# A fused decoder layer on one core: the first dilated head's transposes moved four half items later, and the last norm's inverse root taken from ScalarE and VectorE

## The chip, the core and the metric

The kernel runs on one core of a Trainium2 chip. The core has a matrix engine (TensorE, PE in the profile; its weight loads are listed as PEld), a vector engine (VectorE, DVE), a scalar engine (ScalarE, ACT), a general engine (GpSimd, POOL) and SyncE (SP), which here does nothing but issue transfers. Each engine works through a list of its own in order and waits on semaphores for the others. Transfers (DMA) are issued by SP, by GpSimd and in a few places by ScalarE; each of these has a queue of its own. The metric is the device time of one execution in microseconds (us).

## The reference, cut to what matters

One layer with batch 1, 512 tokens and width 1024, all in fp32. Three attention branches work in parallel, their outputs are gated and merged, and then come a norm, an MLP and a second norm:

```python
proj = x @ w_in                                  # q, k, v of three branches, gates
o_da = diff_attention(...)                       # 4 heads, two softmax maps each
o_sb = stick_breaking_attention(...)             # 8 heads
o_dl = dilated_attention(...)                    # 4 head slots x 3 groups
merged = sum(sigmoid(gate_i) * (o_i @ w_branch_i))
x = layer_norm(alpha * x + merged @ w_out, ln1_g, ln1_b)
c = square(relu(x @ w_up)) @ w_down              # 1024 -> 4096 -> 1024
ple = sigmoid(x @ w_ple_gate) * (p @ w_ple)
x = layer_norm(alpha * x + c + ple, ln2_g, ln2_b)
```

In the dilated branch three groups of keys (windows of 128, 512 and 2048 at strides of 1, 4 and 16) have a softmax each, and the outputs of the three are combined by their denominators:

```python
logits = where(valid, q @ k.T * dh ** -0.5 + bias, -inf)    # per group
lse = logsumexp(logits); o = exp(logits - lse) @ v
wts = softmax(stack(lses)); out = sum_g wts[g] * o[g]
```

The norm is the usual one; the inverse root in it is what the second part of the change computes in another way:

```python
mu = x.mean(-1); var = square(x - mu).mean(-1)
y = (x - mu) * rsqrt(var + 1e-5) * g + b
```

## The kernel before, in words

**Split products.** fp32 matrices are multiplied in pieces. A matrix is split into a high part (rounded, type fp32r) and the remainder, and a product is the sum of three matmuls: high by high, high by remainder, remainder by high. The weights come in blocks of 128 x 1024. SP loads them into a ring of buffers named `raw`; ScalarE casts the high part `wh` (L214), VectorE subtracts it to get the remainder `wl` (L216). A cast may begin only when TensorE has done its last matmul on the older weights in that place of the ring.

**Items.** The heavy work is a list of `items`. An item is a set of weight blocks, a function that emits its matmuls into a bank of PSUM (TensorE's accumulators), and an evacuation that copies or adds the bank into SBUF. The main loop goes through the list: it splits the blocks that come next, emits the evacuation of the item before, then the matmuls of this one. PSUM has two banks named `mm` and six named `at`.

**Value products.** The values of the dilated groups are computed by `value_pair` with a scheme of seven block products in place of eight, in the order 2, 1, 7, 6, 4, 5, 3, each for two halves of the tokens. One such item is twelve matmuls (L426 to L428: high by high, high by remainder, remainder by high, four times). The inputs of products 7, 6, 4 and 5 are sums and differences of blocks of x, made by the generator `value_forms`: VectorE subtracts (L369, L394 and their neighbours; tiles `fr`), ScalarE casts the high part (L239; `u7h`, `u6h` and so on), VectorE takes the remainder (L240; `u5l` and so on). L437 is a copy of a finished bank by ScalarE, L440 an addition by VectorE. After the seven products come ordinary value products on `xhT`, which is x itself.

**Side work.** The attention heads are Python generators. Beside the items the main loop calls `step()`, which moves each active generator on to its next `yield`; it is called before an item, and in the longer items again in the middle. An item of `value_pair` counts as half an item (size 0.5) and has one step, so that there one yield is one half item of twelve matmuls. What a generator emits in a step lies in each engine's list at that place, between the matmuls of the item. A helper then orders each engine's list; it can move single instructions against the order in which they were written.

**A dilated head.** `dil_head(hd)` makes the logits of its three groups, takes the exponentials, and combines the denominators: a matmul with `fold` and a few small VectorE instructions (L1646 to L1655; `mxx`, `ex`, `ot`), in the middle an exponential on ScalarE (L1650). The result `mxx` scales the eight tiles of probabilities: four `L0` tiles (L1657) and four `L12` tiles (L1661). Then TensorE transposes them, seven tiles for `pt0` (L1676, into two banks: five and two by the order of TensorE's list) and eight for `pt12` (L1685), and later multiplies them with the values (L1697, L1702). Between the scaling and the transposes stands one `yield` in every head, and for head 0, the first to run, two more, that is, three half items in all.

**The MLP and the last norm.** The MLP goes through 4096 hidden columns in eight parts up (L1010 copies a part of `up` out of PSUM) and down (L1076 to L1078). The last matmuls fill four token blocks; the last block is done in three pieces, listed in `ends`. When the third piece has been added and its statistics taken, `last_norm` runs (L1213): VectorE aggregates the statistics (L1216), adds epsilon (L1218), GpSimd takes the power -0.5 (L1219), while VectorE subtracts the mean and multiplies by the gain in two halves (L1221). Then three instructions multiply by the root and add the offset (L1224), each followed by its own transfer out (L1226), which is issued by SP, ScalarE and SP.

**Tables of ScalarE.** ScalarE's functions come from tables that have to be loaded. The kernel loads one at the start, and one more in the middle, for the sigmoid of the gates (L507). The root of the norms is taken by GpSimd throughout.

**Loads by GpSimd.** Sums of weight blocks for the seven-product schemes are made in memory by accumulating transfers on GpSimd's queue (L914, L916), all through the kernel. `lows` is the list of all weight remainders in the order in which they were emitted.

Of the kernel before, what the change touches and what calls it, by code (L numbers as in the profile page):

```python
# [14 lines left out]
OP = mybir.AluOpType  # L15
# [42 lines left out]
def trunk(tc, a, out):  # L58
    nc = tc.nc
    es = ExitStack()  # L60
    with es:
# [1094 lines left out]
        def plain(cs, c2, c4, kept):  # L1156

            sums, held = {}, []
            s6 = slot("bn6e")[:, :18].rearrange("p (a b) -> p a b", b=6)

            ends = [(0, slice(0, 512)), (1, slice(0, 256)), (1, slice(256, 512))]

            def part(tt, half, cc):
                n = cc.stop - cc.start
                r = tt % 2
                p, cp = {(0, 0): (2, c2), (1, 0): (4, c4)}.get((tt // 2, half), (0, []))

                def mm(ps):
                    for c, m in zip(cp, (5, 6)):
                        down_mm(ps, m, p, r, c, p == 2 and m == 5, False)  # L1170
                    for i in range(4):
                        h, lo = left[ND - 1, tt // 2, i % 2]
                        q = slice((i // 2) * 256 + r * P, (i // 2) * 256 + r * P + P)
                        c = cs[i % 2, half]
                        s = slice((i // 2) * 512 + cc.start, (i // 2) * 512 + cc.stop)
                        nc.tensor.matmul(ps[:, :n], h[:, q], c["h"][:, s], start=i == 0 and not p, stop=False,
                                         skip_group_check=True)
                        nc.tensor.matmul(ps[:, :n], h[:, q], c["l"][:, s], start=False, stop=False,
                                         skip_group_check=True)
                        nc.tensor.matmul(ps[:, :n], lo[:, q], c["h"][:, s], start=False, stop=i == 3,  # L1180
                                         skip_group_check=True)

                def ev(ps):
                    t = acc[tt, half]
                    if tt < 3:
                        if not half:
                            sums[tt] = small("lsm", 2)
                        nc.vector.scalar_tensor_tensor(t, t, 1.0, ps, op0=OP.mult, op1=OP.add,
                                                       accum_out=sums[tt][:, half:half + 1])
                        if half:  # L1190
                            def fin(h, y):
                                (nc.sync if h else nc.scalar).dma_start(
                                    out[0, tt * P:tt * P + P, 512 * h:512 * h + 512], y)
                            rest = layer_norm_act([acc[tt, 0], acc[tt, 1]], sums[tt], "ln2_g", "ln2_b", fin)
                            if tt == 2:
                                held.append(rest)
                            else:
                                rest()
                        return
                    i = nc.vector.tensor_add(t[:, cc], t[:, cc], ps[:, :n])  # L1200
                    if held:
                        with tc.issue_after(getattr(i, "ins", i)):
                            held.pop()()
                    nc.vector.bn_stats(s6[:, ends.index((half, cc)), :], t[:, cc])
                    if (half, cc) == ends[2]:
                        last_norm()
                free = list(cp) if p and r else []
                if (tt, half, cc) == (3, *ends[2]):
                    free = list(cs.values())
                item(free, mm, ev, need=list(cs.values()) + list(cp),  # L1210
                     bank=(lambda: kept["y", r]) if p == 4 else at_bank if tt == 3 else None)

            def last_norm():  # L1213
                ts = [acc[3, 0], acc[3, 1]]
                mv = small("mv", 2)
                nc.vector.bn_aggr(mv, s6)  # L1216
                r = small("lr", 1)
                nc.vector.tensor_scalar(r, mv[:, 1:2], EPS, None, op0=OP.add)  # L1218
                nc.gpsimd.tensor_tensor(r, r, mhalf, OP.pow)  # L1219
                for h in range(2):  # L1220
                    nc.vector.scalar_tensor_tensor(ts[h], ts[h], mv[:, 0:1], lnc["ln2_g"][h], op0=OP.subtract,  # L1221
                                                   op1=OP.mult)
                for i, (h, cc) in enumerate(ends):
                    nc.vector.scalar_tensor_tensor(ts[h][:, cc], ts[h][:, cc], r, lnc["ln2_b"][h][:, cc],  # L1224
                                                   op0=OP.mult, op1=OP.add)
                    (nc.scalar if i == 1 else nc.sync).dma_start(  # L1226
                        out[0, 3 * P:4 * P, 512 * h + cc.start:512 * h + cc.stop], ts[h][:, cc])

            for tt in range(3):
                for half in range(2):  # L1230
                    part(tt, half, slice(0, 512))
            for half, cc in ends:
                part(3, half, cc)
# [342 lines left out]
        def dil_head(hd):  # L1576
# [83 lines left out]
                o = L12[c // 2][:, (c % 2) * 256:(c % 2) * 256 + 256]  # L1660
                nc.vector.tensor_scalar(o, o, mxx[:, c:c + 1], None, op0=OP.mult)  # L1661
            yield
            if hd == 0:
                yield
                yield

            src0 = {}
# [89 lines left out]
        for n, it in enumerate(items):  # L1757
            if n == last_plain - 1:
                while any(k not in ready for k in range(4, 8)):
                    step()  # L1760
                split_oT(1)
            if n == v_from[0]:
                pending.append(value_forms())
            if n == forms_at:
                pending.append(mixer_forms())
            if n == pairs_at[0] + 3:
                while active or waiting:
                    step()
            if n == pairs_at[2] + 4:
                split_oT(2)  # L1770
            if n == pairs_at[5] + 4:
                split_oT(0)
            need = it["need"] or it["c"]
            while any("h" not in c for c in need):
                pump(freed, 1)
            if prev is not None:
                prev[0]["ev"](prev[1])
                todo, lead = prev[0].get("then", ((), 0))
                preps.extend(todo)
                for _ in range(lead):  # L1780
                    left_step(*preps.popleft())

            pump(freed, {1: 3, 3: 0, 4: 0, wout_at + 8: 0, wout_at + 9: 0}.get(n, 1 if n < 10 else 2))
            if n == 8:
                tie.clear()
            if n == 4:
                with tc.issue_after(st["load"]):
                    load_consts()
            if n == 10:
                with tc.issue_after(st["low"]):  # L1790
                    make_lam()
            if n == 9:
                load_onehot()
            if n == 13:
                pending.append(tables())

            if 12 <= n < wout_at - 6:
                credit += it["size"] * (RATES[0] if n < pairs_at[0] else RATES[1])
            elif n > wout_at + 22:
                credit += 1 / 3  # L1800
            while credit >= 1:
                credit -= 1
                next(sum_steps_, None)
            if n == 22:
                turn_tables()
            if n == DA_TABS:
                da_tables()
            if n == DA_TABS + 4:
                turn_da()
            if n == wout_at + 1:  # L1810
                load_pT()
            if n == wout_at + 5:
                with tc.issue_after(st["added"]), tc.issue_after(st["cast"]):
                    split_pT()
            if n == wout_at - 1:
                load_xn(0)
                load_xn(1)
                ln_consts("ln1_g", "ln1_b")
            if n == ln2_at[0]:
                ln_consts("ln2_g", "ln2_b")  # L1820
            if n > 1:
                step()
            ps = it["bank"]() if it["bank"] else mm_bank()
            for _ in it["mm"](ps) or ():
                if HALF:
                    step()
            plain_left[0] -= n < last_plain
            freed += len(it["c"])

            pump(freed, 0 if n < 10 or wout_at + 7 <= n <= wout_at + 9 else 2)  # L1830
            prev = (it, ps)
            if n + 1 < len(items) and n >= wout_at and pending:
                pass
# [112 lines left out]
```

## Time and profile before

| | |
|---|---|
| median of 3 runs | 1065.49 us (1064.94 to 1065.59) |
| the profiled execution's own time | 1065.99 us |
| its span | 1064.3 us |
| TensorE busy | 1046.7 us, 5802 matmuls |
| VectorE busy | 776.6 us, 1383 instructions |
| ScalarE busy | 568.9 us, 991 instructions |
| GpSimd busy | 146.2 us, 224 instructions |
| moved by DMA | 219.75 MB |

The span runs from the first recorded instruction to the last; the execution's own time has what lies around it in addition. Times inside the trace count from the start of the span. In a line of the timeline stand the start, the length of the whole group, the engine, the line of the kernel, the operation, the tiles (out<-in), the size and the number of instructions; in brackets the wait in front and what ended it. A line of the list of waits gives, for a line of the kernel and the one that it waited for, the sum of the waits, their number and the longest. In a table of windows stand the bounds, the length, the busy time of TensorE, its weight loads, VectorE, ScalarE and GpSimd (with the number of instructions), the clock granted to TensorE as a share of full speed, the busy share of the DMA engines and GB/s. TensorE's matmuls overlap, so a matmul's listed length is longer than the distance from one to the next.

### The profile page before, as it was taken

Reading aid. Unit: us, or ns where it says so; the run is one execution under the profiler, and the core shown is the slowest. Engines: PE = TensorE matmul, PEld = TensorE weight load, DVE = VectorE, ACT = ScalarE, POOL = GpSimd, SP = SyncE. Lnnn points to the kernel's source line nnn. Section 1 sums busy time; section 2 is a strip of 40 time slices with the busy share of each in tenths; the row PEclk is TensorE's granted clock in tenths of the full one; section 3 lists DMA queues with packets and bytes.
Section 4 is the critical chain, followed back from the end, with each engine's and each line's share of the span. In section 5 each row is a group of like instructions: output and inputs, shape, how many; then the busy total and the mean of one; then the engine's idle time right before and its main releaser. Section 6 shows DMA issues by size and latency. Waiting matters only on the chain.

```text
span 1064.3 us, 15603 instructions
## 1 busy us (share of the span) xinstructions
PE 1046.7 (98%) x5802; PEld 903.7 (85%) x5802; DVE 776.6 (73%) x1383; ACT 568.9 (53%) x991; POOL 146.2 (14%) x224
## 2 busy tenths in 40 slices
PE   9999999998999999999999999999999999999996
PEld 6887788887888888888899988888999889889885
DVE  6888667668763757769768773888677877877965
ACT  6665545535442545547545452675656665666651
POOL 0002402220311103230111130100101100100000
PEclk9999999999999999999999999999999999999999
DMA  8346867976996819882676693248888978777602
GB/s 317 110 150 224 186 184 188 311 257 175 304 302 173 233 36 299 235 237 80 210 186 200 176 321 114 63 139 294 239 289 265 238 242 278 234 237 235 196 23 79
DMA packets 63260, 219.75 MB, mean 206 GB/s; under 512 B 7912, under 2 KB 8824, under 8 KB 63184
## 3 DMA queue, kind: packets, MB, share of 16 engines
q1 hardware_dynamic: 37056, 126.80, 34.9%
q0 software_dynamic: 25552, 91.04, 32.6%
q8 instruction: 45, 0.74, 0.3%
q10 hardware_dynamic: 576, 0.92, 0.2%
q14 instruction: 31, 0.25, 0.1%
HBM read 216.61 MB, written 81.81 MB: 280 GB/s over the span
## 4 chain that ended last, share of the span: by engine, by line
PE 88%; DVE 6%; issue 2%; ACT 2%; DMA 0%; POOL 0%; SPq 0%; DVEq 0%; POOLq 0%; ACTq 0%
PE mm L89 13%; PE mm L91 13%; PE mm L90 13%; PE at L89 4%; PE at L1077 4%; PE at L1076 4%; PE at L1078 4%; PE at L91 4%; PE at L90 4%; DVE wl L216 2%; PE mm L458 2%; PE mm L460 2%; PE mm L459 2%; PE at L1467 1%; PE at L133 1%
## 5 line engine op out<-in xcount | busy, mean ns | idle before, releaser
L214 ACT CAST wh<-raw 128x1024 fp32r<-128x1024 f32 x249 | 256.7, 1035 | 254.0 <-PE mm L90 153.5
L216 DVE TENSOR_TENSOR wl<-raw,wh 128x1024 fp32r<-128x1024 f32 x249 | 298.7, 1205 | 102.9 <-ACT wh L214 100.1
L89 PE MATMUL mm<-xhT,wh 128*128 128x512 f32 x368 | 146.8, 399 | 0.0
L91 PE MATMUL mm<-xhT,wl 128*128 128x512 f32 x368 | 144.4, 392 | 0.0
L90 PE MATMUL mm<-xlT,wh 128*128 128x512 f32 x368 | 144.0, 391 | 0.0
L91 PEld LDWEIGHTS mm<-xhT,wl 128*128 128x128 f32 x368 | 69.1, 188 | 14.7
L89 PEld LDWEIGHTS mm<-xhT,wh 128*128 128x128 f32 x368 | 69.3, 188 | 13.6 <-issue 0.4
L90 PEld LDWEIGHTS mm<-xlT,wh 128*128 128x128 f32 x368 | 69.2, 188 | 12.8
L1076 PE MATMUL at<-wh,hh 128*128 128x512 f32 x188 | 73.7, 392 | 0.0
L1077 PE MATMUL at<-wl,hh 128*128 128x512 f32 x188 | 73.7, 392 | 0.0
L89 PE MATMUL mm<-x1hT,wh 128*128 128x256 f32 x256 | 73.7, 288 | 0.0
L1078 PE MATMUL at<-wh,hl 128*128 128x512 f32 x188 | 73.1, 389 | 0.0
L90 PE MATMUL mm<-x1lT,wh 128*128 128x256 f32 x256 | 72.3, 283 | 0.0
L91 PE MATMUL mm<-x1hT,wl 128*128 128x256 f32 x256 | 71.9, 283 | 0.0
L89 PEld LDWEIGHTS mm<-x1hT,wh 128*128 128x128 f32 x256 | 48.8, 190 | 4.7 <-ACT up L1010 2.7
L90 PEld LDWEIGHTS mm<-x1lT,wh 128*128 128x128 f32 x256 | 48.9, 191 | 1.5
L914 POOL DMA_DIRECT2D usum<-in_wu_dram x32 | 28.5, 892 | 153.5 <-DVE wl L216 130.5
L91 PEld LDWEIGHTS mm<-x1hT,wl 128*128 128x128 f32 x256 | 48.6, 191 | 0.0
L914 POOL DMA_DIRECT2D dsum<-in_wd_dram x28 | 25.1, 895 | 127.7 <-DVE wl L216 108.4
L1078 PEld LDWEIGHTS at<-wh,hl 128*128 128x128 f32 x188 | 35.3, 188 | 7.6
L1076 PEld LDWEIGHTS at<-wh,hh 128*128 128x128 f32 x188 | 35.5, 189 | 6.0
L1077 PEld LDWEIGHTS at<-wl,hh 128*128 128x128 f32 x188 | 35.5, 189 | 5.6
(516 smaller groups left out, 2664.1 us busy)
## 6 DMA issues: line engine op xcount, KB each, us to landing
usum<-in_wu_dram POOLq DMA_DIRECT2D x48, 512.0 KB, 7.5
raw<-in_wt_dram SPq DMA_DIRECT2D x46, 512.0 KB, 5.0
dsum<-in_wd_dram POOLq DMA_DIRECT2D x42, 512.0 KB, 7.8
raw<-usum SPq DMA_DIRECT2D x32, 512.0 KB, 4.5
raw<-dsum SPq DMA_DIRECT2D x28, 512.0 KB, 4.9
raw<-in_wd_dram SPq DMA_DIRECT2D x25, 512.0 KB, 4.5
raw<-in_wu_dram SPq DMA_DIRECT2D x24, 512.0 KB, 5.0
raw<-in_wv_dram SPq DMA_DIRECT2D x18, 512.0 KB, 8.1
```

Source lines behind the costliest of these rows:

```text
L89: nc.tensor.matmul(ps, wh, xh, start=start, stop=False, skip_group_check=True)
L90: nc.tensor.matmul(ps, wh, xl, start=False, stop=False, skip_group_check=True)
L91: nc.tensor.matmul(ps, wl, xh, start=False, stop=stop, skip_group_check=True)
L214: i = nc.scalar.copy(h, raw)
L216: i = nc.vector.tensor_sub(lo, raw, h.bitcast(F32))
L458: nc.tensor.matmul(ps, x1, c["h"][:, s], start=k == 0, stop=False)
L459: nc.tensor.matmul(ps, x1, c["l"][:, s], start=False, stop=False)
L460: nc.tensor.matmul(ps, x2, c["h"][:, s], start=False, stop=k == 7)
L914: i = nc.gpsimd.dma_start(o, i, accum_op=OP.add, max_dma_last_dim=4096)
L1076: nc.tensor.matmul(ps, h[:, q], c["h"][:, s], start=go, stop=False, skip_group_check=True)
L1077: nc.tensor.matmul(ps, h[:, q], c["l"][:, s], start=False, stop=False, skip_group_check=True)
L1078: nc.tensor.matmul(ps, lo[:, q], c["h"][:, s], start=False, stop=end, skip_group_check=True)
```

## The change

There are two parts. In `dil_head` the wait of head 0 between the scaling of the tiles and their transposes grows from two extra yields to six, so that the transposes and all that follows in this head's generator come four half items later in the list.

In `last_norm` GpSimd's power is gone. VectorE now computes hv = -(var + eps)/2. ScalarE takes y = sqrt(-2 hv), the root itself. VectorE takes the reciprocal of y, and improves it by one Newton step, r = y (1.5 + y hv y), in two instructions. `center(h)` holds the subtraction of the mean and the multiplication by the gain, as before; the first half is emitted ahead of the reciprocal and the second half behind the Newton step. The three instructions that use r are as they were.

A square root needs another table in ScalarE. So that it is loaded earlier, a square root of a column of the identity matrix, whose result nobody reads, is put at the item `ln2_at[0]`, near the end of the MLP, and tied behind the newest weight remainder emitted there.

```diff
@@ last_norm
-                r = small("lr", 1)
-                nc.vector.tensor_scalar(r, mv[:, 1:2], EPS, None, op0=OP.add)
-                nc.gpsimd.tensor_tensor(r, r, mhalf, OP.pow)
-                for h in range(2):
+                hv, y, r = [small("lr", 1) for _ in range(3)]
+                nc.vector.tensor_scalar(hv, mv[:, 1:2], EPS, -0.5, op0=OP.add, op1=OP.mult)
+                nc.scalar.activation(y, hv, AF.Sqrt, scale=-2.0)
+
+                def center(h):
                     nc.vector.scalar_tensor_tensor(ts[h], ts[h], mv[:, 0:1], lnc["ln2_g"][h], op0=OP.subtract,
                                                    op1=OP.mult)
+                center(0)
+                nc.vector.reciprocal(y, y)
+                nc.vector.scalar_tensor_tensor(r, y, hv, y, op0=OP.mult, op1=OP.mult)
+                nc.vector.scalar_tensor_tensor(r, r, 1.5, y, op0=OP.add, op1=OP.mult)
+                center(1)
                 for i, (h, cc) in enumerate(ends):
                     nc.vector.scalar_tensor_tensor(ts[h][:, cc], ts[h][:, cc], r, lnc["ln2_b"][h][:, cc],
                                                    op0=OP.mult, op1=OP.add)
@@ dil_head
             yield
-            if hd == 0:
-                yield
+
+            for _ in range(6 if hd == 0 else 0):
                 yield
@@ the main loop
             if n == ln2_at[0]:
+
+                i = nc.scalar.activation(small("rt", 1), ident[:, 0:1], AF.Sqrt)
+                tc.add_manual_dep(getattr(i, "ins", i), lows[-1].name, mybir.DependencyInfo(
+                    mybir.DependencyClass.Sync, mybir.DependencyReason.DATA), reason="behind the last gate")
                 ln_consts("ln2_g", "ln2_b")
```

## The prediction

> **What bounds the kernel now.** I read the page first: busy time of each engine, the granted clock by slices, the chain that ended last.
>
> ```profile
> span 1064.3 us, 15603 instructions
> PE 1046.7 (98%) x5802; PEld 903.7 (85%) x5802; DVE 776.6 (73%) x1383; ACT 568.9 (53%) x991; POOL 146.2 (14%) x224
> PE 88%; DVE 6%; issue 2%; ACT 2%; DMA 0%; POOL 0%; SPq 0%; DVEq 0%; POOLq 0%; ACTq 0%
> ```
>
> TensorE carries 88% of the chain. So an edit in the middle of the kernel is worth the TensorE time that it removes, and an edit behind the last matmul is worth what it does to VectorE's chain. Next comes the list of waits, TensorE's own, longest first:
>
> ```profile
> PE at L1676 <- DVE L L1657: 3.7, 2, 3.5
> PE at L1246 <- DVE zero L1243: 1.3, 1, 1.3
> PE at L314 <- ACT wh L214: 1.2, 1, 1.2
> PE at L1537 <- DVE lg L1532: 0.6, 2, 0.4
> ```
>
> The two in the middle belong to the start. The longest wait by far stands at the transposes of a dilated head (L1676), which wait for VectorE's scaling of the L tiles (L1657). The timeline of TensorE puts it at 255 us, and the table of windows shows what follows it:
>
> ```profile
> 254.95 0.39 PE L428 MATMUL mm<-wh,u7l 128*128 128x512 f32 x1
> 258.88 1.14 PE L1676 MATMUL at<-ident,L 128*128 128x128 f32 x7 [3.54 <-DVE L L1657]
> 259.77 0.48 PE L426 MATMUL at<-wh,u7h 128*128 128x512 f32 x1
> ...
> 261.06 0.63 PE L427 MATMUL at<-wl,u7h 128*128 128x512 f32 x1
> ...
> 264.20 1.03 PE L1685 MATMUL at<-ident,L 128*128 128x128 f32 x8
> 264.99 0.48 PE L426 MATMUL mm<-wh,u6h 128*128 128x512 f32 x1
> 265.31 0.39 PE L427 MATMUL mm<-wl,u6h 128*128 128x512 f32 x1
> ...
> 281.43 0.40 PE L426 MATMUL at<-wh,xhT 128*128 128x512 f32 x1
> ```
>
> ```profile
> 240.00:255.00 15.00, 15.00 (x76) 14.36 (x74) 11.91 (x44) 9.73 (x24) 1.66 (x2) 1.00 0.45 117
> 255.00:259.00 4.00, 0.46 (x3) 0.14 (x1) 3.58 (x13) 0.22 (x1) 0.81 (x1) 1.00 1.03 250
> 259.00:264.00 5.00, 5.00 (x19) 3.92 (x19) 4.92 (x12) 2.41 (x4) 0.00 (x0) 0.66 1.04 288
> 264.00:282.00 18.00, 18.00 (x85) 15.11 (x84) 13.36 (x17) 9.34 (x13) 6.06 (x9) 1.00 0.94 254
> ```
>
> The number before the last two of a window is the granted clock: 1.00, 1.00 through the gap, then 0.66 over 259 to 264, then 1.00. The gap costs twice: TensorE stands, and then runs slow.
>
> **Part one, the transposes of head 0.** Matmuls start 0.227 us apart at full clock (71 of them from 265.31 to 281.43). The last one before the gap ends its slot at 254.95 + 0.23 = 255.18. From there to 281.43 pass 26.25 us. The work in them: seven items of twelve matmuls, 84 x 0.227 = 19.07; seven transposes 0.89 (258.88 to 259.77); eight 0.79 (264.20 to 264.99); a switch back from transposes costs 0.32 - 0.23 = 0.09, twice. That is 20.94, so 5.31 us are lost: 3.70 standing, and 1.61 in the item from 259.77 to 264.20, which takes 4.43 in place of 12 x 0.227 + 0.09 = 2.82.
>
> In the changed program TensorE's order after 255.18 is: the second item on u7, eight matmuls of one u6 item, twelve of the other, the four left over, five transposes, a u4 item, two transposes, the other u4 item, eight transposes, the u5 items. The rest of TensorE's list is the same, but for one six-matmul swap near 979 us. So the transposes are reached after 36 matmuls, at 255.18 + 36 x 0.227 = 263.35. There is one switch more, 0.09. If nothing new is waited for, the gain is 5.31 - 0.09 = 5.2 us.
>
> Whether something is depends on VectorE, whose list changes too: in front of the L tiles now stand four subtractions (L394), one weight split (L216) and one split of u5 (L240). Before, they came behind or later:
>
> ```profile
> 257.08 0.16 DVE L1649 TENSOR_TENSOR ex<-ot,mxx 128x8 f32<-128x8 f32 x1
> 257.53 0.17 DVE L1651 TENSOR_TENSOR mxx<-ex,st 128x8 f32<-128x8 f32 x1 [0.28 <-ACT ex L1650]
> ...
> 258.45 1.07 DVE L1657 TENSOR_SCALAR L<-L,mxx 128x128 f32<-128x128 f32 x4
> 259.44 1.14 DVE L1661 TENSOR_SCALAR L<-L,mxx 128x256 f32<-128x256 f32 x4
> 260.49 2.23 DVE L394 TENSOR_TENSOR fr<-xr 128x256 f32<-128x256 f32 x4
> 262.64 1.46 DVE L240 TENSOR_TENSOR u5l<-fr,u5h 128x512 fp32r<-128x512 f32 x2
> 264.35 1.23 DVE L216 TENSOR_TENSOR wl<-raw,wh 128x1024 fp32r<-128x1024 f32 x1 [0.25 <-ACT wh L214]
> ```
>
> Worked out from these: VectorE is free at 257.15. Four L394 take 2.15, the five small instructions from L1651 on 0.92 (257.53 to 258.45), the split 1.14 to 1.23, one L240 0.73, the four L1657 0.99 (258.45 to 259.44). The first L tiles are done at 257.15 + 2.15 + 0.92 + 1.2 + 0.73 + 0.99 = 263.1 if nothing overlaps; the small instructions' waits for each other are now filled with L394, so 262.6 is likelier. TensorE comes at 263.35. Slack 0.2 to 0.7, no wait; the L tiles of the later eight transposes are wanted only at 270.7.
>
> ScalarE is the other cover. Its list now has two casts in front of a PSUM copy (L437) for which the u6 item on the old bank waits, and these casts wait until TensorE is done with the weights of the u7 item. I take the release from the same pair of steps:
>
> ```profile
> 268.96 0.39 PE L428 MATMUL at<-wh,u6l 128*128 128x512 f32 x1
> ...
> 269.39 1.06 ACT L214 CAST wh<-raw 128x1024 fp32r<-128x1024 f32 x1 [1.69 <-PE at L428]
> ```
>
> The cast starts 0.43 after the start of the last matmul that reads the old weights. The u7 item's sixth starts at 256.32, its twelfth at 257.68: first cast 256.75 to 257.8, the exponential of the head, second cast 258.1 to 259.15, copy done at about 259.65 (0.6, like L437's own instances). TensorE wants the bank after 20 matmuls, at 259.72. This is the tightest place: 0.07 us. I cost it at 0, with 0.5 as the upper bound, which is a whole copy late.
>
> The moved transposes issue no DMA. SP's list keeps its order; the loads behind the two earlier splits go out some 4 us sooner, with TensorE. On GpSimd's queue one load of the shift table goes out two issues later; its four tiles are first read 30 us on. TensorE's list of waits above names no tile that a DMA fills after the start, so I carry the 5.2 us to the end unshortened.
>
> **Part two, the early square root.** A ScalarE instruction and a table load are added near 975 us. The price is in the one load in the middle of the kernel:
>
> ```profile
> 481.29 0.61 ACT L239 CAST oTh<-oT 128x512 fp32r<-128x512 f32 x1
> 481.92 1.28 ACT L507 ACT_TABLE_LOAD   x1
> ...
> 975.33 0.36 ACT L1010 COPY up<-mm 128x256 f32<-128x256 f32 x1
> 978.20 1.05 ACT L214 CAST wh<-raw 128x1024 fp32r<-128x1024 f32 x1 [2.51 <-PE mm L90]
> 979.15 0.37 ACT L1010 COPY up<-mm 128x256 f32<-128x256 f32 x1
> ```
>
> It goes into the 2.51 us in which ScalarE waits: 975.70 + 1.28 = 976.98, and 0.2 for the instruction. The second L1010 copy now comes before the cast, so it is done by about 978.7, and TensorE's next matmul into that bank comes, by the new order, at about 978.84. Cost 0. Without that idle time it would be 1.5 us of ScalarE. The cast behind it comes 0.4 us later; its weights are read after 990.
>
> The Trainium skill (ScalarE: Activation LUTs, What ACT_TABLE_LOAD costs) gives a switch of tables about 2.66 us, a load of 1283 ns and a drain of 1380 ns, and so speaks against this edit. The trace agrees with the load, not with the drain: the cast before the load ends at 481.90 and the load starts at 481.92. With the page's figure the copy would be done at about 978.9 and TensorE would wait 0.1, which makes the forecast 1060.9.
>
> **Part three, the last norm.** The tail, from the timeline:
>
> ```profile
> 1055.60 0.24 DVE L1216 BATCH_NORM_AGGREGATE mv<-bn6e 128x2 f32<-128x18 f32 x1
> 1055.87 0.15 DVE L1218 TENSOR_SCALAR lr<-mv 128x1 f32<-128x1 f32 x1
> 1055.94 1.41 DVE L1221 SCALAR_TENSOR_TENSOR xn<-xn,mv,ln_g 128x512 f32<-128x512 f32 x2
> 1056.11 0.98 POOL L1219 TENSOR_TENSOR lr<-lr,mhalf 128x1 f32<-128x1 f32 x1 [5.63 <-DVE lr L1218]
> 1057.26 1.54 DVE L1224 SCALAR_TENSOR_TENSOR xn<-xn,lr,ln_b 128x512 f32<-128x512 f32 x3
> ```
>
> GpSimd's power ends at 1057.09, VectorE's two L1221 at 1057.35. The power is hidden already; removing it frees nothing. New on VectorE: a reciprocal and two small products, 128x1. The square root (about 0.2 us, starting near 1056.06) is done before the first L1221 ends its slot, so the reciprocal does not wait. It costs some 0.1 between two large instructions; the two products depend on each other and the last steps on them, 0.2 each, as the small steps above (five in 0.92). Sum +0.5 us. Bounds: three at 0.07, the distance from L1218 to L1221, +0.2; all three with full waits and a square root 0.2 late, +0.9.
>
> **Sum.** 1065.99 is the profiled execution's own time (span 1064.3), 0.50 above the median 1065.49. 1065.99 - 5.2 + 0 + 0.5 = 1061.3; against the median 1065.49 - 4.7 = 1060.8, 0.44% less.
>
> **Rivals.**
> First, part of the stall comes back at the new place: the additions on VectorE are 2.15 + 1.2 + 0.73 = 4.1 us in front of the L tiles, against 0.7 of slack at most. If they are 2 us late, the gain shrinks to 3.2 and the time is 1062.8 with the clock whole. The trace shows no gap between 0.6 and 3.5 us, so I cannot say from rows whether 2 us would halve the clock; if so, 1064.4. Speaking against it: every one of those instructions has its inputs early.
> The Trainium skill (TensorE: Matmul & The Clock Gate, What's actually happening) puts the slow clock behind an idle window of about 3.4 us. The gap of 3.54 us here agrees; by that rule a gap of 2 us leaves 1062.8.
>
> Second, the move does not do what it says: the whole stall and the slow stretch stand again behind the u6 items, the L tiles being 3.7 us behind TensorE. Then 1065.49 + 0.09 + 0.5 = 1066.1. For this the L chain must end at 267, 4 us past my sum.
>
> Third, slower: the bank for the second u6 item. TensorE waits for the L437 copy, the copy for two casts, these for TensorE. A stall of s here, if over 3.5 us, brings the slow stretch as well (1.6). The kernel ends slower than before once s + 1.6 passes 4.7, so from s = 3.5 (with the gap's price, 5.1) on: 1060.8 + 5.1 = 1065.9; over 0.2% slower from s = 5.3, 1067.7. The casts' inputs landed long before; only a ScalarE queue some 5 us late does this, and ScalarE is busy 2.41 of 5 us there.
>
> **How the numbers follow.** Forecast as summed: 0.77, with a range of its own of 1060.2 to 1061.5. First rival 0.12, second 0.06, third 0.05. About 0.2% (2.1 us) is what a measurement of this kernel tells from no change. Faster than 1063.36: the forecast and most of the first rival, 0.87. Within 0.2%: the second rival, the first with a halved clock and a mild third, 0.09. Slower: 0.04. The range runs from 1059.9 (tail +0.2, no switch cost, and half a microsecond of spread between executions) to 1063.2, which takes in most of the first rival and leaves the other two out.
>
> **What would show it.** Right: TensorE's list of waits without the 3.5 us row, clock 1.00 between 255 and 282, the first matmul on xhT after the u5 items at about 276.2 in place of 281.43; a table load of 1.28 us near 976 without a wait at TensorE behind it; L1224's successor 1.7 to 2.4 us after the aggregate's start, in place of 1.66. Wrong: a wait at the transposes for L or at the u6 item for L437, a window with a clock under 1.00 after 259, or waits at weights after 282.

## The result, and the profile after

The changed kernel takes 1058.38 us (median of 6 runs, 1057.74 to 1058.83) against 1065.61 for the kernel before in the same runs: a ratio of 0.9931, with a 95% interval of 0.9918 to 0.9944. That is 7.2 us less, where 4.7 were forecast, and below the range. First the head of the page, then TensorE's waits (sum, number, longest), then the windows over the place of the old stall:

```profile
span 1056.6 us, 15598 instructions
PE 1044.4 (99%) x5802; PEld 902.8 (85%) x5802; DVE 775.6 (73%) x1386; ACT 570.4 (54%) x994; POOL 145.3 (14%) x223
```

```profile
PE at L314 <- ACT wh L214: 1.4, 1, 1.4
...
PE at L1683 <- DVE L L1664: 0.2, 1, 0.2
```

```profile
255.00:259.00 4.00, 4.00 (x19) 3.30 (x18) 4.00 (x12) 2.21 (x4) 0.80 (x1) 1.00 1.03 252
259.00:264.00 5.00, 5.00 (x26) 4.03 (x25) 5.00 (x15) 4.30 (x9) 1.77 (x2) 1.00 1.05 291
264.00:282.00 18.00, 18.00 (x85) 15.88 (x84) 15.15 (x20) 7.02 (x9) 5.41 (x9) 1.00 1.05 296
```

The transposes (now L1683) no longer wait 3.5 us (the 0.2 left in that row stood behind 300 us in the kernel before, too, and still does), TensorE is busy throughout these windows, and the granted clock is 1.00 where it was 0.66. The timeline of VectorE at the end of the kernel, after:

```profile
1049.90 0.24 DVE L1216 BATCH_NORM_AGGREGATE mv<-bn6e 128x2 f32<-128x18 f32 x1
...
1050.24 0.74 DVE L1223 SCALAR_TENSOR_TENSOR xn<-xn,mv,ln_g 128x512 f32<-128x512 f32 x1
1050.90 0.15 DVE L1226 RECIPROCAL lr<-lr 128x1 f32<-128x1 f32 x1
1050.97 0.73 DVE L1223 SCALAR_TENSOR_TENSOR xn<-xn,mv,ln_g 128x512 f32<-128x512 f32 x1
1051.62 0.21 DVE L1227 SCALAR_TENSOR_TENSOR lr<-lr,lr 128x1 f32<-128x1 f32 x1
1051.87 0.16 DVE L1228 SCALAR_TENSOR_TENSOR lr<-lr,lr 128x1 f32<-128x1 f32 x1
1052.07 1.54 DVE L1231 SCALAR_TENSOR_TENSOR xn<-xn,lr,ln_b 128x512 f32<-128x512 f32 x3
```

The aggregate starts at 1049.90 in place of 1055.60: 5.7 us of the gain lie before it. From it to the last three instructions pass 2.17 us, where it was 1.66: the norm's own chain is 0.5 longer, as forecast. The span is 7.6 us shorter (7.7 by the rounded figures of the pages), which leaves 2.4 us to be found behind the last instruction. They are in a part that the working had not looked at, the instructions that close the program. They all carry the line of the kernel's outermost block, L1942 before and L1953 after. A row gives their number, the shortest, the middle and the longest in ns, and the start of the first and of the last. Before:

```profile
L1942 POOLq EVENT_SEMAPHORE  x4: 17/17/17, 1063.5 to 1064.2; - x4
L1942 POOLq DRAIN  x3: 46/102/7396, 1056.1 to 1064.0; - x3
L1942 SPq DRAIN  x3: 7/7/7, 1061.0 to 1063.7; - x3
```

After:

```profile
L1953 POOLq EVENT_SEMAPHORE  x4: 17/17/17, 1055.9 to 1056.5; - x4
L1953 POOLq DRAIN  x3: 46/93/6952, 1044.1 to 1056.4; - x3
L1953 SPq DRAIN  x3: 7/7/7, 1055.8 to 1056.1; - x3
```

An engine's first closing drain stands behind the last instruction of its list, SP's also behind its waits for the last transfers out, the last of which lands at 1060.8 in the kernel before. There SP is through at 1061.0. But GpSimd, which runs the closing exchange of semaphores, starts it only at 1063.5, because its own first drain, begun at 1056.1 beside the power of the norm, takes 7.396 us and ends at 1063.5. The power itself ends at 1056.11 + 0.98 = 1057.09; the drain goes on for 6.4 us behind it. After, GpSimd's last instruction is the power of the norm one token block earlier:

```profile
1044.16 0.54 POOL L703 TENSOR_TENSOR lr<-lr,mhalf 128x1 f32<-128x1 f32 x1 [7.41 <-DVE lr L702]
```

It ends at 1044.70. The drain takes the same 6.4 us behind it, and is over at 1051.1, long before SP at 1055.8; the exchange starts 0.1 later. So the exchange stands 0.1 us behind SP's drain, where it stood 2.5 behind it. The sum: -5.7 + 0.5 - 2.4 = -7.6. The medians differ by 7.2; the profiled execution of the kernel before was 0.4 above its median (1065.99 against 1065.61).

### The profile page after: what moved, and what is told of

Same layout as the page of the kernel before. It is cut to its first block, busy times and chain, and to the rows that moved or that the text cites. A ratio compares the mean times of both kernels' runs of the same rounds, so it can differ in the third digit from the quotient of the medians.

```text
span 1056.6 us, 15598 instructions
## 1 busy us (share of the span) xinstructions
PE 1044.4 (99%) x5802; PEld 902.8 (85%) x5802; DVE 775.6 (73%) x1386; ACT 570.4 (54%) x994; POOL 145.3 (14%) x223
## 3 DMA queue, kind: packets, MB, share of 16 engines
q0 software_dynamic: 25552, 91.04, 32.9%
## 4 chain that ended last, share of the span: by engine, by line
PE 89%; DVE 6%; issue 2%; ACT 1%; DMA 0%; POOL 0%; SPq 0%; DVEq 0%; POOLq 0%; ACTq 0%
PE mm L89 14%; PE mm L91 13%; PE mm L90 13%; PE at L89 4%; PE at L1076 4%; PE at L1077 4%; PE at L1078 4%; PE at L91 4%; PE at L90 4%; DVE wl L216 2%; PE mm L458 2%; PE mm L460 2%; PE mm L459 2%; PE at L1474 1%; PE at L133 1%
## 5 line engine op out<-in xcount | busy, mean ns | idle before, releaser
L216 DVE TENSOR_TENSOR wl<-raw,wh 128x1024 fp32r<-128x1024 f32 x249 | 298.6, 1205 | 99.4 <-ACT wh L214 96.9
```

What stands on the lines that cost most here:

```text
L216: i = nc.vector.tensor_sub(lo, raw, h.bitcast(F32))
```

## The experiments

Two theories are to be told apart. A: the end waits for GpSimd's closing drain. B: all of the surplus comes from the middle, and the norm costs 0.5 as forecast. The diffs show only the lines that matter.

### Each part of the change alone

The first kernel is the kernel before with only this edit; the second is the changed kernel with it undone.

```diff
-            if hd == 0:
-                yield
+            for _ in range(6 if hd == 0 else 0):
                 yield
```

> The kernel before with the six yields alone; the last norm keeps GpSimd's power. Theory A (the closing drain): GpSimd's list ends with a drain that takes 6.4 us from the end of its last instruction, the power of the last norm, and the end of the program waits for it. Then this kernel keeps the whole end of the kernel before, 8.65 us from the start of the aggregate to the end of the span, and wins only what TensorE wins, 5.2 to 5.7 us: 1060.0. Theory B (the middle): the move of the transposes is worth some 7.7 us and the norm costs 0.5 as forecast. Then 1057.9.

> The changed kernel with the two extra yields of before: the last norm and the early square root alone. Theory A: the end shrinks from 8.65 to 6.75 us from the aggregate on, TensorE's part is as before: 1063.7. Theory B: 0.5 slower than before, 1066.1.

Measured: the move alone 1060.23 us (ratio 0.9945, 0.9932 to 0.9957), the norm alone 1063.66 (0.998, 0.997 to 0.9989), both against 1065.93. Theory A has both, theory B is off by 2.3 and 2.4 us. The norm (with its early square root), which was to cost half a microsecond, wins 2.3 by itself; in its trace the drain is over at 1055.9, long before SP at 1060.6, and the exchange starts at 1060.7. In the move alone the drain is where it was, behind the power:

```profile
1050.47 0.98 POOL L1219 TENSOR_TENSOR lr<-lr,mhalf 128x1 f32<-128x1 f32 x1 [5.64 <-DVE lr L1218]
```

```profile
L1942 POOLq EVENT_SEMAPHORE  x4: 17/17/17, 1057.9 to 1058.5; - x4
L1942 POOLq DRAIN  x3: 46/93/7394, 1050.4 to 1058.3; - x3
L1942 SPq DRAIN  x3: 7/7/7, 1055.4 to 1058.1; - x3
```

The power ends at 1051.45 and the exchange starts 6.4 us later, 2.5 us behind SP.

### One late instruction of GpSimd, whose result nobody reads

```diff
                 nc.scalar.activation(y, hv, AF.Sqrt, scale=-2.0)
+                nc.gpsimd.tensor_tensor(small("idle", 1), mv[:, 1:2], mhalf, OP.pow)
```

and, in the second kernel, in its place

```diff
+                nc.gpsimd.tensor_copy(small("idle", 1), mv[:, 1:2])
```

> The changed kernel with one GpSimd power more, of the variance of the last norm into a tile that nobody reads, right behind the square root. Theory A: the power ends some 1.3 us behind the start of the aggregate, the drain 6.4 behind that, and 0.8 go to the end: 8.5 us in place of 6.75, so 1060.1, with GpSimd's drain the last thing to end. Theory B: nobody waits for the power, 1058.4.

> The same with a copy of 128x1 by GpSimd in place of the power. Theory A, if the drain is that of any GpSimd instruction: it ends some 6.4 us behind the copy, which is about 0.7 us sooner than behind the power: 1059.4. Theory A, if the drain is that of the power alone: 1058.4. Theory B: 1058.4, the drain short or not waited for.

Measured: 1060.11 us (0.9943, 0.993 to 0.9955) and 1059.54 (0.994, 0.9926 to 0.9953). Nothing waits for these instructions but the end, and against the changed kernel's 1058.38 they give back 1.7 and 1.2 us. Instruction and closing rows, the copy first, then the power:

```profile
1049.93 0.74 POOL L1221 COPY idle<-mv 128x1 f32<-128x1 f32 x1 [5.58 <-DVE mv L1216]
```

```profile
L1954 POOLq EVENT_SEMAPHORE  x4: 17/17/17, 1057.1 to 1057.7; - x4
L1954 POOLq DRAIN  x3: 46/102/7134, 1049.9 to 1057.6; - x3
L1954 SPq DRAIN  x3: 7/7/7, 1055.5 to 1057.3; - x3
```

```profile
1050.12 1.10 POOL L1221 TENSOR_TENSOR idle<-mv,mhalf 128x1 f32<-128x1 f32 x1 [5.58 <-DVE mv L1216]
```

```profile
L1954 POOLq EVENT_SEMAPHORE  x4: 17/17/17, 1057.6 to 1058.3; - x4
L1954 POOLq DRAIN  x3: 46/93/7507, 1050.1 to 1058.1; - x3
L1954 SPq DRAIN  x3: 7/7/7, 1055.7 to 1057.9; - x3
```

The copy ends at 1050.67, the power at 1051.22, and both drains go on for 6.4 us; the exchange starts 1.6 and 1.9 us behind SP's drain. So the drain does not need the power: a copy of 128x1, as late, brings it as well. With the kernels above this shows theory A.

### What the drain is the price of

Four small programs leave the layer out: SP loads 128x1024, VectorE halves it twenty times, SP stores it four times, and GpSimd copies one column at the end. They differ in what GpSimd transferred before: another 128x1024, in one, 64 or 128 pieces, which VectorE adds to the first. The program without transfers has neither the loop nor the addition. Their times say nothing of the layer's, and each ran once, so the scatter of their figures is not known.

```diff
+        for i in range(LOADS):          # 1, 64, 128
+            c = 1024 // LOADS
+            nc.gpsimd.dma_start(w[:, i * c:(i + 1) * c], x[1, :, i * c:(i + 1) * c])
+        nc.vector.tensor_add(t, t, w)
```

> A program that leaves nearly everything of the layer out: SP loads 128x1024, VectorE halves it twenty times, SP writes it out four times, and GpSimd copies one column of it at the end. GpSimd's queue carries no transfer at all. If the closing drain is a fixed cost of GpSimd, it again ends 6.38 us after the copy. If it is the price of transfers that GpSimd has issued before, it takes well under 1 us.

> The small program (all of the layer left out but a load, a halving and a store) with one load of 128x1024 issued by GpSimd ahead, and the copy of one column by GpSimd at the end. If the closing drain is paid as soon as GpSimd has issued any transfer, it ends 6.4 us after the copy, as in the layer; if it grows with the number of transfers, it stays well under 1 us.

> The same with the load cut into 64 transfers of 128x16. If the drain is paid once for any transfer, 6.4 us, as with one; if it grows with the number of transfers, it is a good part of 6.4 us here and some sixty times what one transfer gives.

> The small program with the load cut into 128 transfers of 128x8. The drain took 0.07 us behind the copy without a transfer, 0.16 with one, 5.31 with 64, and 6.38 in the layer with 202. If it grows with every transfer (0.082 each) it takes 10.6 us here, and the layer's 202 must differ in kind; if it grows up to a ceiling it takes 6.3 to 6.4, as in the layer.

The copy and the drain with no transfer, then the same two rows with 64:

```profile
18.62 0.18 POOL L22 COPY s<-t 128x1 f32<-128x1 f32 x1 [18.18 <-DVEq L35]
```

```profile
L35 POOLq DRAIN  x3: 34/77/271, 18.6 to 25.7; - x3
```

```profile
52.63 0.18 POOL L24 COPY s<-t 128x1 f32<-128x1 f32 x1 [17.48 <-DVE t L20]
```

```profile
L37 POOLq DRAIN  x3: 40/102/5519, 52.6 to 59.7; - x3
```

| transfers issued by GpSimd | 0 | 1 | 64 | 128 | the layer's 202 |
|---|---|---|---|---|---|
| drain behind the last instruction, us | 0.07 | 0.16 | 5.31 | 1.88 | 6.38 |

Without transfers of its own GpSimd's drain costs next to nothing here, and one transfer adds 0.09. So the small programs show that it is not a fixed price of the engine but comes with its transfers. That the layer's 6.4 us are of the same kind is inferred: no run takes the transfers out of the layer. They need not be under way: with 64 the copy comes 17 us after the last issue, and its input needs the loads; in the layer's kernel before GpSimd's last transfer lands at 965.2, 91 us ahead of the drain. Nor does the drain simply grow with their number: 128 gave less than 64, so both my guesses for 128 were wrong. The packets that GpSimd's queue carried do not order it either: 144, 2048, 4096, and 25552 in the layer. In what way it counts stays open. In the layer it was 6.4 us in all nine kernels.

### The early square root

```diff
             if n == ln2_at[0]:
-                i = nc.scalar.activation(small("rt", 1), ident[:, 0:1], AF.Sqrt)
-                tc.add_manual_dep(...)
                 ln_consts("ln2_g", "ln2_b")
```

> The changed kernel without the early square root whose result nobody reads: the table for the square root is then loaded in front of the last norm's own root. Theory C, the load waits with the root for VectorE: the root is done 1.28 us later, the reciprocal waits for it, and the end comes some 1.0 us later: 1059.4. Theory D, the load goes ahead as soon as ScalarE has issued its last transfer, near 1047.7, and is done by 1049.0, ahead of the root at 1050.4: 1058.4, and the early root wins nothing.

Measured: 1059.27 us (0.994, 0.9926 to 0.9953). ScalarE's timeline at the end:

```profile
1046.95 0.34 ACTq L1192 DMA_DIRECT2D out_dram<-xn  x1
1050.06 1.28 ACT L1220 ACT_TABLE_LOAD   x1 [7.29 <-DVE lr L1219]
1051.35 0.20 ACT L1220 ACTIVATE lr<-lr 128x1 f32<-128x1 f32 x1
```

VectorE's, of the same kernel:

```profile
1049.55 0.24 DVE L1216 BATCH_NORM_AGGREGATE mv<-bn6e 128x2 f32<-128x18 f32 x1
...
1049.89 1.40 DVE L1223 SCALAR_TENSOR_TENSOR xn<-xn,mv,ln_g 128x512 f32<-128x512 f32 x2
1051.59 0.16 DVE L1226 RECIPROCAL lr<-lr 128x1 f32<-128x1 f32 x1 [0.29 <-ACT lr L1220]
...
1052.23 1.54 DVE L1231 SCALAR_TENSOR_TENSOR xn<-xn,lr,ln_b 128x512 f32<-128x512 f32 x3
```

Theory C: though ScalarE has nothing to do, the load does not go ahead, it waits with the root. From the aggregate to the last three instructions it is now 2.68 us in place of 2.17, so by the trace the early root is worth 0.5 us. 1.0 was expected; part of the load is hidden because the second half of the subtraction moved in front of the reciprocal. The medians show 0.9, but the runs of either kernel scatter by about as much (0.8 and 1.1 us).

### The Newton step

```diff
-                nc.vector.reciprocal(y, y)
-                nc.vector.scalar_tensor_tensor(r, y, hv, y, op0=OP.mult, op1=OP.mult)
-                nc.vector.scalar_tensor_tensor(r, r, 1.5, y, op0=OP.add, op1=OP.mult)
+                nc.vector.reciprocal(r, y)
```

> The changed kernel without the Newton step: the reciprocal of the square root is used as it is, so the two small products between the reciprocal and the last three instructions are left out and the inverse root is less accurate. If the small products stand on the path as forecast (0.25 and 0.20 in the timeline) and the closing drain of GpSimd is long done, the end comes 0.45 us sooner: 1057.9. If the drain or something else ends last now, 1058.4.

Measured: 1057.77 us (0.9927, 0.9914 to 0.9939).

```profile
1049.83 0.23 DVE L1216 BATCH_NORM_AGGREGATE mv<-bn6e 128x2 f32<-128x18 f32 x1
...
1051.55 1.54 DVE L1229 SCALAR_TENSOR_TENSOR xn<-xn,lr,ln_b 128x512 f32<-128x512 f32 x3
```

1.72 us in place of 2.17: the two dependent products of 128x1 cost 0.45, on the path, where the forecast priced them at 0.2 each. Its median is the lowest here, with the Newton step left out of the root (what that does to the root's accuracy was not measured); its interval overlaps that of the changed kernel.

### A gap between the two that the trace knew

```diff
-            for _ in range(6 if hd == 0 else 0):
+            for _ in range(4 if hd == 0 else 0):
```

> The changed kernel with four extra yields in place of six. The order of ScalarE and VectorE is that of the changed kernel up to the L tiles, but TensorE takes the u6 item on the old mm bank straight after the u7 items, so it waits for the copy L437 from 257.75 to about 259.55: a gap of 1.8 us, between the 0.6 and the 3.5 us that the trace of before shows. The L tiles are then ready when TensorE comes to them. If such a gap leaves the clock whole, 1060.2; if it halves the clock as the gap of 3.5 us did, 1061.8 with a window under 1.00 after 259.

Measured: 1060.34 us (0.9949, 0.9937 to 0.9962). TensorE's longest wait, and the windows:

```profile
PE mm L426 <- ACT dl_v L437: 1.6, 1, 1.6
```

```profile
255.00:259.00 4.00, 3.14 (x14) 2.25 (x12) 4.00 (x11) 1.99 (x3) 0.81 (x1) 1.00 1.02 220
259.00:264.00 5.00, 4.24 (x22) 3.61 (x23) 5.00 (x16) 3.68 (x8) 1.77 (x2) 1.00 1.04 274
```

The bank that the prediction called the tightest place is late here by 1.6 us, for a reason of order alone: TensorE comes to it 8 matmuls sooner. The clock stays at 1.00 through and after it, so this gap costs about its own length (from the last u7 matmul on the first bank to the first on `xhT` pass 22.89 us in place of 21.14), where the one of 3.54 us cost 1.6 more.

## Why the prediction was wrong

**Part one held, to 0.15 us.** Forecast 5.2. From the end of the last u7 matmul before the old gap to the first on `xhT` it was 26.25 us; after, 20.91 (254.81 + 0.23 = 255.04 to 275.95), where 20.94 + 0.09 were worked out. The places on the way:

```profile
254.81 0.39 PE L428 MATMUL mm<-wh,u7l 128*128 128x512 f32 x1
...
259.56 0.47 PE L426 MATMUL mm<-wh,u6h 128*128 128x512 f32 x1
...
263.31 0.71 PE L1683 MATMUL at<-ident,L 128*128 128x128 f32 x5
...
275.95 0.40 PE L426 MATMUL at<-wh,xhT 128*128 128x512 f32 x1
```

```profile
258.91 0.58 ACT L437 COPY dl_v<-mm 128x512 f32<-128x512 f32 x1
```

```profile
261.27 1.11 DVE L1664 TENSOR_SCALAR L<-L,mxx 128x128 f32<-128x128 f32 x4
```

The transposes come at 263.31 (forecast 263.35), the L tiles in front of them are done by 262.3 (262.6). The copy ends at 259.49 and its bank is taken at 259.56, with the 0.07 of slack that the prediction gave it and no wait. So the first rival, the second and the third did not happen. Some of this closeness is luck. The slack is smaller than the errors of single terms: the sum counts seven transposes as 0.89 us, what they took right behind the gap, and here they take 0.60 (263.31 to 263.77 and 266.61 to 266.75); and the first matmul on the u6 bank stands 0.32 ahead of the next, where 0.23 was counted. The 5.7 us before the aggregate are 0.4 more than the 5.34 of this stretch: 0.14 of it lies before the stretch and 0.22 behind it, and no run here tells it from the scatter of executions.

The first rival's open question is answered in part by the kernel with four yields: a gap of 1.6 us leaves the clock whole. No run here has a gap between 1.6 and 3.5. The Trainium skill (TensorE: Matmul & The Clock Gate, What's actually happening) needs an idle window of about 3.4 us for the slow clock. Both gaps of this case agree: 3.54 us was followed by a clock of 0.66, 1.62 us by one of 1.00.

**Part two held.** The table load found its idle time, and TensorE has no wait there:

```profile
969.85 0.36 ACT L1010 COPY up<-mm 128x256 f32<-128x256 f32 x1
970.24 1.28 ACT L1828 ACT_TABLE_LOAD   x1
971.53 0.20 ACT L1828 ACTIVATE rt<-ident 128x1 f32<-128x1 f32 x1
972.85 0.37 ACT L1010 COPY up<-mm 128x256 f32<-128x256 f32 x1 [1.12 <-PE mm L91]
```

The load starts 0.03 us after the copy before it ends and the activation 0.01 us after the load, so the drain that the prediction weighed against it does not show here either.

**Part three failed, in one sentence.** "The power is hidden already; removing it frees nothing." Against VectorE that was right, and +0.5 for VectorE's new chain was measured as +0.51. But the power had a second follower beside VectorE's last three instructions: the closing drain of its own engine, 6.4 us, which ended 2.5 us behind SP's drain for the last transfer out. Taking the power away moved GpSimd's last instruction from 1056.11 to L703 at 1044.16, 12 us earlier, of which 5.7 are time won before the last norm. With that the drain lies beside other work. The term was +0.5 and measured -1.9 (0.5 less 2.4), and that is the miss of 2.4: 1060.8 against 1058.4. None of the rivals was a faster one, and the lower end of the range left room only for a cheaper chain of VectorE, for the switch and for the spread between executions.

The sign could have been had from the kernel before. Its last three instructions on VectorE end at 1057.26 + 1.54 = 1058.80, and the span at 1064.3. The prediction carried these 5.5 us as a constant, without asking which engine ended last in them.

## What to carry to other kernels

Work the path through to the last row of the span, not to the last instruction that computes: what each engine does between its last instruction and the closing exchange belongs to the sum. A kernel that issues transfers through GpSimd should give that engine nothing to do near the end; here even a copy of 128x1 that nobody read cost 1.2 us. By these figures the drain is free if GpSimd's last instruction ends more than 6.4 us before SP's closing drain; in the changed kernel it ends 11 us before, and no run lies near that bound. How long the drain is has to be read in the kernel's own trace, for in the small programs it was between 0.07 and 5.31. When a stall is moved, count for every engine what now stands in front of the waited-for tile; here that gave the new times to a few tenths.

## What the runs showed of the hardware that was not expected

- GpSimd's closing drain went on for 6.4 us behind its last instruction in the layer, behind the power and behind the copy alike, and for 0.07 us in a program in which GpSimd had issued no transfer. The number of transfers alone does not give its length (64: 5.31, 128: 1.88).
- A table load in front of an idle ScalarE's activation waited for that activation's input (idle 7.29 us, then 1.28 for the load).
- GpSimd's work on 128x1 was longer beside some of VectorE's: the power took 0.98 and 1.10 us beside the subtractions of the last norm, and 1.46 and 1.47 in two of the seven L703 of the kernel before, both begun beside an L216; in the other five it took 0.54 to 0.57. One of these five stands beside an L742, which reads one of its inputs from a PSUM bank, so not every instruction of VectorE goes with it. The copy took 0.74 in the last norm against 0.18 in the small program. No run tests VectorE as the cause by itself.
